# A two-layer decoder trunk on one core: two early requests moved, the convolution's columns and the token-major copy of x

## The chip, the core and the metric

The kernel runs on one core of a Trainium2 chip. The time is the device time of one execution in microseconds (us), as the median of several executions. Five engines work side by side, each through its own instruction queue in the order in which the program was written: TensorE (PE, with its weight loads shown as PEld), VectorE (DVE), ScalarE (ACT), GpSimd (POOL) and SyncE (SP). SP computes nothing; it only requests transfers. ACT and POOL request some as well.

## What is computed

The reference is a decoder trunk of two layers over 256 tokens of width 1024. The first layer mixes tokens by a causal convolution of 31 taps, the second by block attention; beside both runs a cross-attention into 256 memory tokens. A residual with layer norm, a mixture of 32 experts (two per token) and another residual with layer norm follow. The change touches the first layer alone, before its mixture:

```python
u = jnp.dot(x, conv_w_in[j])
y_mix = conformer_conv(u[..., :2 * MIX_WIDTH], conv_dw_w[j], conv_dw_b[j], conv_ln_g[j], conv_ln_b[j])
q_mem = u[..., 2 * MIX_WIDTH:]
...
y = jnp.dot(jnp.concatenate([y_mix, y_mem], axis=-1), w_o[i])
x = layer_norm(DEEPNORM_ALPHA * x + y, ln1_g[i], ln1_b[i])
```

`conformer_conv` gates one half of its input by the sigmoid of the other, convolves each channel over time, normalises and applies silu.

## The kernel before

All large tiles live in one pool, `big`, of 22 slots of 1 MB (128 partitions by 2048 floats). A slot holds either a weight tile that SP loads or working data that `act` (L150) takes. The list of wanted loads is fixed at the start (L249 to L274), and `pump` (L137) issues the next load at each point of the program where a slot is sure to be free: `act`, `free` and `done` count slots, and a first pass through the whole program finds how many loads may be out at each point. At the start fourteen loads go out: six tiles of `conv_w_in` ("cv"), the memory `memT`, two tiles of `w_mem_kv` with one more of `conv_w_in` between them, and four tiles of `w_o`. The fifteenth, the gains (L189), takes the slot of `hs` of channel block 0 and so waits for `conv(0)`.

Engines work in the order written by hand. `conv_layer` (L541) does, in this order:

- `parted` (L389) splits x transposed (`raw`, loaded at L248) into a rounded part and a rest, by ACT and DVE; then ACT requests the convolution's columns (taps, bias and gains, 204 KB) into the end of the tile `cv` (L552).
- `feed.ahead` and `feed.take` (L350) split weight tiles by halves in the same way: ACT casts (L344), DVE subtracts (L345), and `three` (L400) multiplies 24 times per half on PE (L405). ACT's first cast stands right behind the request for the columns in ACT's queue.
- `glu(b)` (L574) for b = 0, 1, 2 computes a gated projection of 256 channels: two halves into `p_`, two into `g_`, a sigmoid, a product `h` (L594). POOL then writes `h` to DRAM (`hd`, L597) and `shifted` (L612) reads it back eight times, shifted, as `hs` (L617). In `glu(2)`, `conv(0)` and `conv(1)` (L620) stand between the halves of `p_` and those of `g_`.
- `taps(b)` (L556) multiplies the columns into small diagonal blocks `wdg` on POOL. It stands behind `shifted(b)` in POOL's queue. `conv(c)` multiplies `wdg` with `hs` on PE (L626). `last_taps` (L600) does the remaining taps on DVE, from the columns.
- Behind `glu(2)` follow the projection of the memory, `conv(2)`, `conv(3)`, the queries, the attention scores of two heads with `conv(4)`, then `router_load(0)` (four requests on SP, L327 to L331), the token-major copy of x into `xn` (four requests on SP of 256 KB each, L685), the other scores, `conv(5)`, and `residual` (L498), which multiplies `xn` by a scaled identity into the accumulators of the layer's output (L496). Behind it stand the channel means (L694, L695), the values' projection (L405 again) and the variance (L714). DVE subtracts the means at L701.

The mixture `moe(0)` follows, whose 192 tiles of 1 MB stream through the same slots, and then the second layer.

Of the kernel before, what the change touches and what calls it, by code (L numbers as in the profile page):

```python
# [17 lines left out]
S = 256  # L18
D = 1024
NT = S // 128  # L20
# [5 lines left out]
MC = MIX // 128  # L26
CW = 31
# [50 lines left out]
def trunk(tc, *args):  # L78
    trace = body(Blank(), None, *[Blank() for _ in args])
    for i in range(len(trace) - 1, 0, -1):  # L80
        trace[i - 1] = min(trace[i - 1], trace[i])
    body(tc, trace, *args)
# [3 lines left out]
def body(ctx, tc, ahead, xT0, xs, memT, w_mem_kv, conv_w_in, conv_cols, moba_w_in, w_o, gains, w_r,  # L86
          gain_cols, b_rg, b_re, w_gate, w_up, w_down, out):
    nc = tc.nc
# [11 lines left out]
    def pb():  # L100
        return ps.tile([P, 512], F32, name="pb", tag="pb")
# [4 lines left out]
    def t2(name, dt=F32):  # L106
        return wk.tile([P, 512], dt, name=name, tag="t2", bufs=3)
# [38 lines left out]
    def changed():  # L146
        trace.append(NB - use["a"] + use["done"])
        pump()

    def act(name, dt=F32):  # L150
        use["a"] += 1
        changed()
        return big.tile([P, 2048], dt, name=name, tag="big")

    def free(n=1):
        use["a"] -= n
        changed()
# [5 lines left out]
    def want(key, load, gate=None):  # L163
        todo.append((key, load, gate))
# [4 lines left out]
    def done(key):  # L169
        have.pop(key, None)  # L170
        use["done"] += 1
        changed()
# [7 lines left out]
    def load(src, i):  # L180

        def load_(t_):
            nc.sync.dma_start(t_, src[i])
            return t_
        return load_
# [59 lines left out]
    xn = [[keep.tile([P, 512], F32, name=f"xn{t}{h}") for h in range(2)] for t in range(NT)]  # L245
    raw = act("raw")
    for h in range(2):
        nc.sync.dma_start(raw[:, h * 1024:(h + 1) * 1024], xT0[:, h * 1024:(h + 1) * 1024])  # L248
    for b in range(3):  # L249
        for i in range(2):  # L250
            want(("cv", b, i), load(conv_w_in, 2 * b + i))
# [56 lines left out]
    for g, experts in enumerate(plan):  # L308
        for kind, k, n, lo in experts:
            c = NDYN + k if kind == "s" else k  # L310
# [13 lines left out]
    def router_load(l):  # L324
        rws_ = xt([P, 2, J, NL], "rw")
        rw = rws_[:, 0]
        nc.sync.dma_start(rbias[:, :NG], b_rg[l:l + 1])  # L327
        nc.sync.dma_start(rbias[:, 8:], b_re[l:l + 1])
        nc.sync.dma_start(rw, w_r[l])
        gbc = small([P, 2 * J], "gbc")  # L330
        nc.sync.dma_start(gbc, gain_cols[l])  # L331
        rws.append((rw, rws_[:, 1], gbc))
# [208 lines left out]
    def conv_layer():  # L541
        acc = Acc()
        xT = parted(raw, "xT", (nc.scalar.copy, nc.vector.tensor_copy))
        free()
        cv_ = act("cv")
        cv = cv_[:, :MC * S].rearrange("p (c s) -> p c s", c=MC)
        npc, nwr = MC * (CW + 5), MC * 32
        cols = cv_[:, MC * S:MC * S + npc + nwr]
        pct = cols[:, :npc].rearrange("p (c k) -> p c k", c=MC)
        wrc = cols[:, npc:].rearrange("p (c b q) -> p c b q", c=MC, b=4)  # L550
        id32 = cv_[:, 2048 - 32:]
        nc.scalar.dma_start(cols, conv_cols)  # L552
        hd = dr.tile([MC, P * HW], F32, name="hd")
        wdg, hsrc, hs = {}, {}, {}

        def taps(b):  # L556
            w_ = act("wdg").rearrange("p (n c) -> p n c", c=32)
            nc.gpsimd.tensor_tensor(
                w_, wrc[:, 2 * b:2 * b + 2].rearrange("p c b q -> p (c b q)")[:, :, None].to_broadcast(
                    [P, 64, 32]),  # L560
                id32[:, None, :].to_broadcast([P, 64, 32]), op=OP.mult)
            wdg[b] = w_.rearrange("p (i b q) c -> p i b q c", i=2, b=4)
# [6 lines left out]
        def halves(o, xT, n=2):  # L569
            for i in range(2):  # L570
                proj_T(o[:, i * 256:(i + 1) * 256], feed.take(n), xT)
                free()

        def glu(b):  # L574
            p_ = pb()
            halves(p_, xT)
            if b == 0:
                nc.vector.tensor_reduce(id32, ident.rearrange("p (r c) -> p c r", r=4), axis=AX.X, op=OP.add)
            else:
                last_taps(b - 1)  # L580
            if b == 2:
                conv(0)
                conv(1)
            g_ = pb()
            halves(g_, xT)
            sg = t2("sg")
            nc.scalar.activation(sg, g_, AF.Sigmoid)
            hh = (xt, ot)[b]([P, 2, HW], "h") if b < 2 else None
            for i in range(2):
                h = hh[:, i] if b < 2 else t2("h")[:, :HW]  # L590
                nc.gpsimd.memset(h[:, 0:CW - 1], 0.0)
                nc.gpsimd.memset(h[:, CW - 1 + S:], 0.0)
                k = slice(i * S, (i + 1) * S)
                nc.vector.tensor_mul(h[:, CW - 1:CW - 1 + S], p_[:, k], sg[:, k])  # L594
                hsrc[2 * b + i] = h
            for i in range(2):
                nc.gpsimd.dma_start(hd[2 * b + i].rearrange("(p s) -> p s", p=P), hsrc[2 * b + i])  # L597
            shifted(b)

        def last_taps(b):  # L600

            for c in (2 * b, 2 * b + 1):
                o, h = cv[:, c], hsrc.pop(c)
                for k in range(CW - 1, 4 * NQ - 1, -1):
                    w_ = pct[:, c, k:k + 1]
                    if k == CW - 1:
                        nc.vector.tensor_scalar(o, h[:, k:k + S], w_, pct[:, c, CW + 1:CW + 2], op0=OP.mult,
                                                op1=OP.add)
                    else:
                        nc.vector.scalar_tensor_tensor(o, h[:, k:k + S], w_, o, op0=OP.mult, op1=OP.add)  # L610

        def shifted(n):  # L612

            for c in (2 * n, 2 * n + 1):
                hs[c] = act("hs")[:, :4 * HW].rearrange("p (b s) -> p b s", b=4)
                for r in range(4):
                    nc.gpsimd.dma_start(hs[c][32 * r:32 * r + 32, :, :HW - 4],  # L617
                                        view(hd[c, r:], [[HW, 32], [32 * HW, 4], [1, HW - 4]]))

        def conv(c):  # L620
            p_ = pb()
            w_ = wdg[c // 2][:, c % 2]
            h = hs.pop(c)
            for q in range(NQ):
                for b in range(4):
                    nc.tensor.matmul(p_[32 * b:32 * b + 32, :S], lhsT=w_[:, b, q, :],  # L626
                                     rhs=h[:, b, 4 * q:4 * q + S], start=q == 0, stop=q == NQ - 1)
            nc.vector.tensor_add(cv[:, c], p_[:, :S], cv[:, c])
            free(1 + c % 2)
            if 0 < c < MC - 1:  # L630
                nc.vector.tensor_add(csum, cv[:, c], cv[:, 0] if c == 1 else csum)
# [6 lines left out]
        mT = parted(held("mem"), "mT")  # L638
        done("mem")
        taps(1)  # L640
        glu(2)

        p_ = pb()
# [36 lines left out]
        next(ats[0])  # L680
        conv(4)
        router_load(0)
        for t in range(NT):
            for half in range(2):
                nc.sync.dma_start(xn[t][half], xs[t, half])  # L685
        feed.ahead(2)
        next(ats[1])
        conv(5)
# [727 lines left out]

    second = moba_layer()
    moe(0, conv_layer(), second)
    moe(1, second)
    return trace  # L1420
# [56 lines left out]
```

## Time and profile before

| | us |
|---|---|
| median of three runs | 1175.22 |
| the three runs | 1174.49, 1175.22, 1183.54 |
| the profiled execution | 1182.57 |
| its span, from the first to the last instruction | 1180.9 |

The profile shows one execution. PE is busy for 87% of the span, DVE for 31%, ACT for 18%, POOL for 5%. The convolution layer takes roughly the first 140 us. A timeline row gives start, duration, engine, line, operation, what it writes and reads, and in brackets how long the engine had been idle and what released it. Rows of SPq, ACTq and POOL with DMA_DIRECT2D are requests; a transfer itself ends later ("landing").

### The profile page before, as it was taken

Reading aid. Unit: us, or ns where it says so; the run is one execution under the profiler, and the core shown is the slowest. Engines: PE = TensorE matmul, PEld = TensorE weight load, DVE = VectorE, ACT = ScalarE, POOL = GpSimd, SP = SyncE. Lnnn points to the kernel's source line nnn. Section 1 sums busy time; section 2 is a strip of 40 time slices with the busy share of each in tenths; the row PEclk is TensorE's granted clock in tenths of the full one; section 3 lists DMA queues with packets and bytes.
Section 4 is the critical chain, followed back from the end, with each engine's and each line's share of the span. In section 5 each row is a group of like instructions: output and inputs, shape, how many; then the busy total and the mean of one; then the engine's idle time right before and its main releaser. Section 6 shows DMA issues by size and latency. Waiting matters only on the chain. (4 is left out here: it accounts for less than half of the span.)

```text
span 1180.9 us, 26574 instructions
## 1 busy us (share of the span) xinstructions
PE 1028.2 (87%) x11292; PEld 722.3 (61%) x11292; DVE 366.4 (31%) x936; ACT 210.5 (18%) x456; POOL 60.6 (5%) x152
## 2 busy tenths in 40 slices
PE   1998999999889998866589998999997999996775
PEld 1986766665565575544469986666545656654542
DVE  3576832221121121111065765222211211221103
ACT  2314411111010010001044532011010111110000
POOL 1440200000000000000020002000000000000001
PEclk9999989999999999889899997999998999997777
DMA  9686969999999999999997386999999999999994
GB/s 381 235 282 265 347 251 419 424 424 426 425 424 425 427 424 425 426 426 425 425 427 271 108 293 252 384 425 424 426 427 422 425 427 425 424 426 425 426 425 177
DMA packets 63656, 447.16 MB, mean 379 GB/s; under 512 B 7656, under 2 KB 8040, under 8 KB 10280
## 3 DMA queue, kind: packets, MB, share of 16 engines
q1 hardware_dynamic: 61640, 439.73, 90.2%
q0 software_dynamic: 1600, 4.90, 1.5%
q8 instruction: 92, 1.51, 0.5%
q10 hardware_dynamic: 288, 0.73, 0.2%
q14 instruction: 36, 0.29, 0.1%
HBM read 442.87 MB, written 2.46 MB: 377 GB/s over the span
## 5 line engine op out<-in xcount | busy, mean ns | idle before, releaser
L974 PE MATMUL pb<-w,xg 128*32 128x128 f32 (+2 forms) x6528 | 400.1, 323 | 87.3 <-DMA w<-in_w_gate_dram 51.0
L974 PEld LDWEIGHTS pb<-w,xg 128*32 128x32 f32 (+2 forms) x6528 | 276.6, 123 | 208.9 <-issue 82.8
L1026 PE MATMUL pb<-w,hT 128*32 128x256 f32 (+1 forms) x1600 | 157.5, 432 | 7.8 <-DMA w<-in_w_down_dram 3.1
L1026 PEld LDWEIGHTS pb<-w,hT 128*32 128x32 f32 (+1 forms) x1600 | 74.5, 116 | 62.9 <-issue 36.5
L1031 ACT COPY o<-pb 32x256 f32<-32x256 f32 (+2 forms) x104 | 43.2, 416 | 367.1 <-DVE o L1031 232.5
L405 PE MATMUL pb<-xT,hl 128*128 128x256 f32 x672 | 86.0, 290 | 25.8 <-ACT hl L344 25.6
L1031 DVE COPY o<-pb 32x256 f32<-32x256 f32 (+2 forms) x104 | 49.8, 478 | 177.6 <-PE pb L1026 157.7
L998 DVE TENSOR_TENSOR h<-pb,h 128x128 f32<-128x128 f32 (+2 forms) x64 | 22.9, 358 | 253.8 <-PE pb L974 246.8
L405 PEld LDWEIGHTS pb<-xT,hl 128*128 128x128 f32 x672 | 84.0, 198 | 27.3 <-ACT hl L344 25.6
L496 PE MATMUL pa<-o,pt 128*128 128x512 f32 x192 | 92.7, 628 | 3.5 <-DVE o L1031 2.0
L950 PEld LDWEIGHTS pb<-oh,xn 128*128 128x128 f32 x704 | 80.6, 192 | 7.4 <-issue 7.4
L950 PE MATMUL pb<-oh,xn 128*128 128x128 f32 x704 | 84.0, 278 | 0.0
L345 DVE TENSOR_TENSOR hl<-w,hl 128x1024 fp32r<-128x1024 f32 x53 | 63.1, 1221 | 36.0 <-ACT hl L344 33.1
L496 PEld LDWEIGHTS pa<-o,pt 128*128 128x128 f32 x192 | 37.7, 207 | 44.5 <-issue 32.4
L344 ACT CAST hl<-w 128x1024 fp32r<-128x1024 f32 x54 | 54.7, 1053 | 33.3 <-DMA w<-in_memT_dram 19.3
L992 ACT ACTIVATE h<-pb 128x128 f32<-128x128 f32 (+2 forms) x64 | 21.2, 331 | 195.9 <-PE pb L974 195.0
L128 POOL TENSOR_SCALAR lmv<-lmv 128x1 f32<-128x1 f32 x8 | 1.7, 216 | 1027.7 <-DVE lmv L506 1026.0
L496 PE MATMUL pa<-hl,y 128*128 128x512 f32 x192 | 46.0, 395 | 0.0
L125 DVE COPY hT<-pb 128x128 f32<-128x128 f32 (+2 forms) x32 | 11.4, 358 | 105.1 <-PE pb L1004 81.2
L123 ACT COPY xg<-pb 128x512 f32<-128x512 f32 x22 | 12.9, 586 | 160.4 <-PE pb L950 160.4
L496 PEld LDWEIGHTS pa<-hl,y 128*128 128x128 f32 x192 | 35.5, 188 | 8.0 <-issue 0.5
L1238 DVE TENSOR_SCALAR ow<-iota,sm,sw 128x128 f32<-128x128 f32 x96 | 26.8, 343 | 19.2 <-PEq L1395 13.3
(229 smaller groups left out, 705.9 us busy)
## 6 DMA issues: line engine op xcount, KB each, us to landing
w<-in_w_gate_dram SPq DMA_DIRECT2D x128, 1024.0 KB, 19.5
w<-in_w_up_dram SPq DMA_DIRECT2D x128, 1024.0 KB, 19.5
w<-in_w_down_dram SPq DMA_DIRECT2D x128, 1024.0 KB, 19.5
w<-in_moba_w_in_dram SPq DMA_DIRECT2D x10, 1024.0 KB, 18.4
w<-in_w_o_dram SPq DMA_DIRECT2D x8, 1024.0 KB, 19.8
w<-in_conv_w_in_dram SPq DMA_DIRECT2D x7, 1024.0 KB, 15.4
w<-in_gains_dram SPq DMA_DIRECT2D x4, 1024.0 KB, 12.4
hs<-hd POOLq DMA_DIRECT2D x24, 142.0 KB, 3.2
```

The costliest lines, as they stand in the source:

```text
L123: nc.scalar.copy(o, i)
L344: nc.scalar.copy(hi, src)
L345: eng.tensor_sub(lo, src, hi.bitcast(F32))
L405: nc.tensor.matmul(o, lhsT=lhs(a, j), rhs=rhs(b, j), start=k == 0, stop=k == 3 * n - 1)
L496: nc.tensor.matmul(self.at[t][half], lhsT=lhsT, rhs=rhs, start=start, stop=stop)
L950: nc.tensor.matmul(p_[:, j - jj], lhsT=now(t, j), rhs=oh[t], start=t == 0, stop=t == NT - 1)
L974: nc.tensor.matmul(o_[b * n:(b + 1) * n, :], lhsT=self.xs[:, j, :], rhs=wj[:, pairs(b) if fw == P else slice(b * fw, (b + 1) * fw)], start ...
L992: nc.scalar.activation(self.h[:, :fw], g_, AF.Silu)
L998: nc.vector.tensor_mul(self.h[:, :fw], u_, self.h[:, :fw])
L1026: nc.tensor.matmul(ds[0][b * n:(b + 1) * n, :dw], lhsT=chunk(c), rhs=wd(c, b * dw, (b + 1) * dw), start=c == 0, stop=c == 3)
L1031: (nc.scalar.copy if 2 * b >= m else nc.vector.tensor_copy)(o[lo:lo + n, b * D // m:(b + 1) * D // m], ds[b] if nb == 1 else ds[0][b * n:( ...
L1238: nc.vector.tensor_scalar(o_[:, t], iota, sm[:, i:i + 1], sw[:, 4 + i:5 + i], op0=OP.is_equal, op1=OP.mult)
```

## The change

Two requests move; nothing is added or removed. The tile `cv` is taken, and its columns are requested by ACT, right after x is requested and before any weight tile is. The four requests for `xn` on SP move from behind `router_load(0)` to ahead of `glu(2)`. The number of slots in use is the same from `conv_layer`'s first steps on, so the loads are issued at the same points of the program.

```diff
     raw = act("raw")
     for h in range(2):
         nc.sync.dma_start(raw[:, h * 1024:(h + 1) * 1024], xT0[:, h * 1024:(h + 1) * 1024])
+    cv_ = act("cv")
+    ncol = MC * (CW + 5), MC * 32
+    nc.scalar.dma_start(cv_[:, MC * S:MC * S + sum(ncol)], conv_cols)
     for b in range(3):
         for i in range(2):
             want(("cv", b, i), load(conv_w_in, 2 * b + i))
...
         xT = parted(raw, "xT", (nc.scalar.copy, nc.vector.tensor_copy))
         free()
-        cv_ = act("cv")
         cv = cv_[:, :MC * S].rearrange("p (c s) -> p c s", c=MC)
-        npc, nwr = MC * (CW + 5), MC * 32
-        cols = cv_[:, MC * S:MC * S + npc + nwr]
...
-        nc.scalar.dma_start(cols, conv_cols)
...
         taps(1)
+        for t in range(NT):
+            for half in range(2):
+                nc.sync.dma_start(xn[t][half], xs[t, half])
         glu(2)
...
         conv(4)
         router_load(0)
-        for t in range(NT):
-            for half in range(2):
-                nc.sync.dma_start(xn[t][half], xs[t, half])
         feed.ahead(2)
```

## Rows read from the trace of the kernel before

**Rows 1.** The page's 40 slices: GB/s moved in each slice of 29.5 us.
```profile
GB/s 381 235 282 265 347 251 419 424 424 426 425 424 425 427 424 425 426 426 425 425 427 271 108 293 252 384 425 424 426 427 422 425 427 425 424 426 425 426 425 177
```
**Rows 2.** Waits, 0 to 180 us: total us, times, longest.
```profile
ACT hl L344 <- DMA w<-in_memT_dram: 19.3, 1, 19.3
```
**Rows 3.** Timeline of all engines, 0 to 70 us: the start.
```profile
4.87 0.78 SPq L183 DMA_DIRECT2D w<-in_memT_dram  x1
...
9.40 0.33 SPq L183 DMA_DIRECT2D w<-in_conv_w_in_dram  x1
...
14.26 7.74 SPq L183 DMA_DIRECT2D w<-in_w_o_dram  x4
24.09 0.38 ACTq L552 DMA_DIRECT2D cv<-in_conv_cols_dram  x1
24.50 5.78 ACT L344 CAST hl<-w 128x1024 fp32r<-128x1024 f32 x6 [19.27 <-DMA w<-in_memT_dram]
...
25.60 31.77 PE L405 MATMUL pb<-xT,hl 128*128 128x256 f32 x240 [25.60 <-ACT hl L344]
```
**Rows 4.** DMA requests by tile: count, KB each, median us to landing.
```profile
hs<-hd POOLq DMA_DIRECT2D x24, 142.0 KB, 3.2
...
w<-in_memT_dram SPq DMA_DIRECT2D x1, 1024.0 KB, 19.2
...
cv<-in_conv_cols_dram ACTq DMA_DIRECT2D x1, 204.0 KB, 7.0
```
**Rows 5.** Windows: length, busy us of PE, PEld, DVE, ACT, POOL; PEclk, DMA share, GB/s.
```profile
20.00:30.00 10.00, 4.40 (x20) 4.40 (x21) 4.42 (x4) 5.50 (x6) 0.00 (x0) 1.00 1.01 425
30.00:40.00 10.00, 10.00 (x79) 10.00 (x78) 2.77 (x4) 1.56 (x2) 0.00 (x0) 1.00 1.01 428
...
41.00:42.00 1.00, 1.00 (x11) 1.00 (x10) 0.82 (x3) 1.00 (x2) 0.20 (x1) 1.00 0.09 25
...
100.00:105.00 5.00, 5.00 (x8) 2.02 (x9) 2.34 (x3) 0.77 (x1) 0.00 (x0) 0.66 0.64 240
```
**Rows 6.** Timeline of all engines, 69 to 150 us: PE ahead of and behind the residual.
```profile
99.82 5.40 PE L496 MATMUL pa<-xn,alpha 128*128 128x512 f32 x8 [3.25 <-DMA xn<-in_xs_dram]
...
105.06 0.59 PE L694 MATMUL pb<-csum,avg 128*128 128x256 f32 x2
...
105.73 6.10 PE L405 MATMUL pb<-hl,mT 128*128 128x256 f32 x48
```
**Rows 7.** Timeline of all engines, 0 to 70 us: the first convolution's supply.
```profile
41.80 1.33 POOL L597 DMA_DIRECT2D hd<-h  x2 [37.95 <-DVE h L594]
...
44.72 4.49 POOL L617 DMA_DIRECT2D hs<-hd  x8 [1.57 <-ACT hl L344]
...
49.23 3.67 POOL L558 TENSOR_TENSOR wdg<-cv 128x2048 f32<-128x2048 f32 x1
...
57.30 6.25 PE L626 MATMUL pb<-hs,wdg 128*32 128x256 f32 x112
...
60.59 0.33 SPq L189 DMA_DIRECT2D w<-in_gains_dram  x1
```
**Rows 8.** Tile hs, requests of 75 to 78 us: time to landing.
```profile
DMA to landing us min/median/max: 4.6/7.8/8.0
```
**Rows 9.** Timeline of all engines, 69 to 150 us: SP's requests beside those hs.
```profile
75.28 6.57 SPq L213 DMA_DIRECT2D w<-in_w_up_dram  x2
```
**Rows 10.** PEld's timeline, 99 to 106 us: the last two of eight loads.
```profile
103.77 0.19 PEld L496 LDWEIGHTS pa<-xn,alpha 128*128 128x128 f32 x1 [0.25 <-issue]
104.20 0.19 PEld L496 LDWEIGHTS pa<-xn,alpha 128*128 128x128 f32 x1 [0.24 <-issue]
```
**Rows 11.** Timeline of all engines, 69 to 150 us: DVE and ACT behind the means.
```profile
99.99 2.35 DVE L345 TENSOR_TENSOR hl<-w,hl 128x1024 fp32r<-128x1024 f32 x2
...
106.12 1.08 DVE L701 TENSOR_TENSOR cv<-cv,pb 128x256 f32<-128x256 f32 x3 [3.78 <-PE pb L695]
...
109.48 0.42 ACT L703 ACTIVATE sq<-cv 128x256 f32<-128x256 f32 x1 [0.25 <-DVE cv L701]
```

More of the change, by code (lines that the diff above doesn't have):

```diff
@@ L544, in conv_layer @@
         free()
-        cv_ = act("cv")
         cv = cv_[:, :MC * S].rearrange("p (c s) -> p c s", c=MC)
-        npc, nwr = MC * (CW + 5), MC * 32
-        cols = cv_[:, MC * S:MC * S + npc + nwr]
-        pct = cols[:, :npc].rearrange("p (c k) -> p c k", c=MC)
-        wrc = cols[:, npc:].rearrange("p (c b q) -> p c b q", c=MC, b=4)
+        cols = cv_[:, MC * S:MC * S + sum(ncol)]
+        pct = cols[:, :ncol[0]].rearrange("p (c k) -> p c k", c=MC)
+        wrc = cols[:, ncol[0]:].rearrange("p (c b q) -> p c b q", c=MC, b=4)
         id32 = cv_[:, 2048 - 32:]
-        nc.scalar.dma_start(cols, conv_cols)
         hd = dr.tile([MC, P * HW], F32, name="hd")
```

## Prediction

> **What bounds the kernel now.** I read the page's slices first. From the seventh slice (177 us) to the end, but for a dip between the mixtures, the transfers run at 419 to 427 GB/s [rows 1]: the mixtures are bound by the stream of expert tiles, and in the first six slices, where this change lies, they are not (235 to 381). What the convolution layer saves should therefore reach the end whole: the stream that follows keeps its length and starts earlier, since its requests are released by slots that this layer frees.
>
> Then the waits of the first 180 us. The longest one in front of a moved request is ACT's: 19.3 us before its first cast, by the profile for `memT` [rows 2]; PE's wait for `xn` comes below. The timeline shows what ACT's wait is. ACT's cast stands behind the columns' request, and that comes at 24.09; the cast follows at 24.50 and PE's first matmul at 25.60 [rows 3]. The cast reads a `conv_w_in` tile, not `memT`. It is the request in front of it that waits: `memT` was requested at 4.87 and took 19.2 us [rows 3, 4], so it landed at 24.07, 0.02 us ahead. Counting the requests of SP and ACT together in program order, `memT` is the 9th and the columns are the 17th. SP's 11th comes at 9.40 and its 13th to 16th start at 14.26, spread over 7.74 us [rows 3], about 2.45 us apart, which is what one tile of 1.05 MB takes at 428 GB/s [rows 5]. I read from this that a request waits for the landing of the one eight places before it; then the 11th shows the landing of the 3rd, which is the first weight tile, at 9.40.
>
> PE is the limit from 25.60 to 57.37, without a gap: 240 matmuls, 48 to a weight tile, so 6.35 us per tile of which one lands every 2.45 us [rows 3].
>
> Later PE waits 3.25 us at L496 for `xn`, until 99.82, so it was free at 96.57 [rows 6]. That also costs clock: in 100 to 105 us the granted clock is 0.66, where 30 to 40 us has 1.00 [rows 5].
>
> **The columns.** As third request they wait for no landing. The request itself (0.38 us of ACT) falls in ACT's wait for x. Their 204 KB take 0.49 us at 428 GB/s ahead of the first weight tile, which then lands at 9.89 instead of 9.40. The cast follows at once, and the first matmul 1.10 us after the cast (24.50 to 25.60) [rows 3]: PE starts at 11.0, 14.6 us earlier. If the columns delay the tile by nothing, it is 15.1; if by twice their size, 14.1. Later tiles come faster than PE uses them, so all 240 matmuls move by as much, and would end at 42.8. In program order there are seventeen hardware requests up to here as before, and those behind wait for landings long past.
>
> The cover that this takes away is that of POOL's round trip. In the profile, `h` goes out at 41.80, when the weight tiles have just run out: 25 GB/s in 41 to 42 us against 428 ahead of it [rows 5, 7]. Moved by 14.6 us it goes out at 27.2, into a stream that lasts until 41.2, and until about 43.7 with `xn` behind it (2.45 us, below). Nearest rows for a transfer in such a stream: the columns themselves took 7.0 us for 204 KB with tiles queued around them, and the `hs` requests of 75 to 78 us, with an expert tile requested at 75.28, up to 8.0 [rows 4, 8, 9]; the median of `hs` is 3.2. In the profile the second `hd` needs about 2.2 us (second request at about 42.5, `hs` from 44.72). `wdg` is ready at 52.90 and `conv(0)` starts at 57.30: 4.4 us of slack [rows 7]. With 7.0 us for `hd` the slack falls to -0.4; with 5.5, which I take since `hd` is smaller than the columns, to 1.1: `hs` requested from 33.5 to 38.0, `wdg` at 41.7, `conv(0)` at 42.7. The last `hs`, requested at 37.5, lands by 45.5 even at 8.0, and `conv(1)` wants it at 45.9. For small delays of DVE's work, which POOL's product now meets elsewhere, I take 0.5, with 0 and 1.6 as ends. Blocks 1 and 2 have slack of their own: the second set of `hs` is wanted by `conv(2)`, behind a whole `glu`.
>
> **xn.** Its four requests pass the fifteenth load, the four of `router_load` and eight tiles of the first experts on SP. SP stands idle from 22.0 to 60.59 there, because the gains wait for `conv(0)` [rows 3, 7], so four requests cost SP nothing. They wait for landings of eight before (`memT` and the next three), go out from about 24.5 to 32 behind the last `w_o` tile, and land by 44. The first use is at 96.57 less 14.1, so at 82. PE then runs the eight matmuls without the wait and at full clock. The last two weight loads at full clock are 0.43 us apart [rows 10], so eight take 3.44 us; the matmuls for the means keep their 0.67 (105.06 to 105.73). From 96.57 to the values' projection at 105.73 it is 9.16 us [rows 6], and becomes 4.11: 5.05 us less, of which 3.25 is the wait and 1.80 the clock. If the clock stays low there for another reason, 3.25.
>
> What is late next is DVE: it is occupied with L345 until 102.34 [rows 11], so L701 moves from 106.12 to 102.34, by 3.78 and not by 5.05. But the variance stands behind the 48 matmuls of the projection, which end at 105.73 + 6.10 - 5.05 = 106.8, and the last of ACT's squares, which ended at 109.90, moves with L701 to 106.1 [rows 11]. PE sets the pace with 0.7 us to spare. The megabyte of `xn` also leaves a stretch at 425 GB/s for one in which the queues stood nearly empty; nothing waits on it there, and I count nothing.
>
> **The sum.** 14.6 + 5.05 - 0.5 = 19.1 us. The profiled execution took 1182.57, so 1163.5; it is 7.35 above the median of the three, and against the median of 1175.2 the same sum gives 1156.1.
>
> **Rivals.**
>
> *Turns.* POOL's transfers may get only one turn for each weight tile queued. For it: the `hs` of 75 to 78 us took 8.0 and not 3.2 with few tiles around. Against it: the columns got through seven queued tiles in 7.0 us. Then each of two `hd` waits a turn of 2.45 us, `hs` is requested from about 34.4, four of them land by 45.2, and the rest once the tiles run out at about 44, 0.6 apart. `conv(0)` starts 2.5 us late, and the clock loss behind a wait of that kind was 1.8 at `xn`: 4.3 us off, 1160.4.
> The Trainium skill's page "DMA: Bandwidth & Descriptors", section "Queues, rings and completion order", says that an engine goes round-robin between queues and drains a whole packet of some 9 to 17 descriptors before it switches. By that rule it would be this rival, 1160.4, against 1156.1 by the columns' row.
>
> *Starved.* POOL's transfers get nothing until the tiles run out at 43.7. Then `hd` lands at about 45.2, `hs` is requested until 49.7, `wdg` is ready at 53.4, and `conv(0)` starts there: 3.9 us earlier than before, less 1.8 of clock, with 5.05 from `xn`: 7.1 in all, 1168. For it: the same `hs` row, of which the median is 7.8. Against it: again the columns.
>
> *The columns were not the wait.* If ACT waits for something else that ends at 24.1, only `xn` counts: 1170.2. Against it stands the 0.02 us.
>
> *Slower.* PE's first 20 matmuls took 4.40 us up to 30, 0.22 each; the next ten microseconds have 79, 0.127 each [rows 5]. If the slow pace belongs to what goes on at the start (tiles streaming in) and not to PE's first steps, all 240 take 52.8 us from 11.0: `conv(0)` at 63.9, 6.6 later than before, less 5.05, and the 112 matmuls of the convolution at that pace some 4.6 more: 1177 to 1181. It decides from about 224 slow matmuls on. Against it: from 30 to 40 us tiles stream in at 428 GB/s beside the fast pace.
>
> **How the numbers follow.** My forecast has 0.58 (1152 to 1160 alone, from the bounds of its terms and the scatter of the runs), turns 0.20, starved 0.14, columns not the wait 0.04, slower 0.04. The prediction is 1156. The range reaches from the forecast's lower end past turns to starved, 1151 to 1168, and leaves out half of starved and the last two. About 1% is what a measurement of this kernel can tell from no change: below 1163.5 lie the forecast and most of turns, 0.73; within 1% starved, the columns case and the rest of turns, 0.24; above it only part of the slow pace, 0.03.
>
> **What would show it.** The columns' request within a microsecond of the start; ACT's first cast at 9.9 and PE's first matmul at 11.0; `hd` requested near 27.2; `conv(0)` near 42.7, where PE's idle time ahead of L626 tells the forecast (0), turns (2 to 3) and starved (over 9) apart; no wait at L496 and a granted clock near 1.00 there; the mixture's first matmul 19 us earlier. It would be wrong if ACT's first cast stays near 24, or if PE loses at L626 what it gained.

## The result and the profile after

The changed kernel takes 1165.88 us against 1181.28 for the kernel before, medians of ten executions each: a ratio of 0.987, with a 95% interval from 0.985 to 0.989. That is 15.4 us, of which the interval leaves 13.0 to 17.8. It is faster by over 1%, and inside the predicted range, but 3.7 us short of the 19.1 that the forecast summed up; the rival called turns (14.8 us, from 1175.2 to 1160.4) is nearer. The predicted 1156 is off by 9.9 us: 6.1 of them because it starts from 1175.2, the median of three runs of the kernel before, where ten gave 1181.28, and the rest is the sum.

PE's timeline of the changed kernel, start and duration first, in brackets how long PE had been idle and what released it (the changed kernel's lines are three later than before from L251 to about L550):

```profile
10.68 31.23 PE L408 MATMUL pb<-xT,hl 128*128 128x256 f32 x240 [10.68 <-ACT hl L347]
45.26 7.94 PE L626 MATMUL pb<-hs,wdg 128*32 128x256 f32 x112 [3.35 <-DMA hs<-hd]
53.12 6.02 PE L408 MATMUL pb<-xT,hl 128*128 128x256 f32 x48
...
86.15 3.70 PE L499 MATMUL pa<-xn,alpha 128*128 128x512 f32 x8
89.69 0.59 PE L694 MATMUL pb<-csum,avg 128*128 128x256 f32 x2
...
90.37 6.10 PE L408 MATMUL pb<-hl,mT 128*128 128x256 f32 x48
```

PE starts at 10.68 and not at 25.60 [rows 3], and the wait at the residual is gone, with its slow matmuls: from L499 to the values' projection it is 4.22 us, where it was 5.91 after a wait of 3.25 [rows 6]. New is the wait of 3.35 us ahead of L626, the convolution of block 0. It takes 7.94 us where it took 6.25 [rows 7].

Subtracting start by start shows where the time came from and where some of it went back:

| start of | before | after | difference |
|---|---|---|---|
| the 240 matmuls | 25.60 | 10.68 | -14.92 |
| `conv(0)` | 57.30 | 45.26 | -12.04 |
| the matmuls behind `conv(1)` | 63.48 | 53.12 | -10.36 |
| the values' projection | 105.73 | 90.37 | -15.36 |
| the mixture's first matmul (L1075) | 138.36 | 123.00 | -15.36 |

ACT's part of the changed kernel's start, in the timeline of all engines. The columns' request comes with the first one of SP, and the first cast at the moment (9.57) at which SP, too, sees the first weight tile landed:

```profile
0.85 0.40 ACTq L251 DMA_DIRECT2D cv<-in_conv_cols_dram  x1
0.85 0.86 SPq L248 DMA_DIRECT2D raw<-in_xT_dram  x2
...
9.57 0.33 SPq L183 DMA_DIRECT2D w<-in_conv_w_in_dram  x1
9.58 1.99 ACT L347 CAST hl<-w 128x1024 fp32r<-128x1024 f32 x2 [3.58 <-DMA w<-in_conv_w_in_dram]
...
24.16 8.94 SPq L643 DMA_DIRECT2D xn<-in_xs_dram  x4
...
26.34 1.34 POOL L597 DMA_DIRECT2D hd<-h  x2 [22.49 <-DVE h L594]
33.07 4.38 POOL L617 DMA_DIRECT2D hs<-hd  x8 [5.40 <-DMA hd<-h]
37.47 3.66 POOL L558 TENSOR_TENSOR wdg<-cv 128x2048 f32<-128x2048 f32 x1
```

Between the second `hd` and the first `hs` POOL waited 1.57 us before [rows 7] and waits 5.40 now, inside the stream of weight tiles. `wdg` is ready at 41.13, before PE needs it; what PE waits for is `hs`. The time to landing of these eight `hs`:

```profile
DMA to landing us min/median/max: 6.3/11.1/12.5
```

The median of `hs` before was 3.2 [rows 4], and 7.8 in its worst stretch [rows 8]. The transfers from 37 to 45 us, by queue (q1 holds SP's requests, q0 POOL's; packets, MB, share of the engines):

```profile
q1 hardware_dynamic: 244, 1.71, 71.4%
q0 software_dynamic: 244, 0.75, 30.5%
```

Packet stands against packet, 244 to 244, so in this stretch neither queue is starved, and not every POOL transfer has to wait for a whole tile. Before it, however, the first one does wait about that long. From 33 to 36 us, with six `hs` requested, the queues carried:

```profile
q1 hardware_dynamic: 176, 1.27, 100.2%
q0 software_dynamic: 3, 0.00, 0.1%
```

The first piece of `hs` goes at 36.8, 3.7 us after the request; in the kernel before it went at 46.0, 1.3 us after. The 2.4 us more are about what a tile takes (2.45 us). `hd` is held up alike: no POOL packet goes between its request at 26.34 and 30 us.

Then the sum of both queues is slow. These are the stretches ahead of and inside the sharing, and that of `conv(0)` (length, busy us of PE, PEld, DVE, ACT, POOL, then granted clock, DMA share, GB/s):

```profile
30.00:36.00 6.00, 6.00 (x53) 6.00 (x52) 3.60 (x6) 0.00 (x0) 2.93 (x6) 1.00 1.01 421
36.00:45.00 9.00, 5.90 (x50) 5.70 (x48) 8.01 (x6) 5.62 (x6) 6.46 (x10) 1.00 1.02 321
45.00:50.00 5.00, 4.75 (x58) 3.13 (x62) 3.22 (x7) 1.05 (x1) 0.00 (x0) 0.66 1.03 317
```

Busy all the time, the queues move 321 GB/s in place of 421. Most of that drop is not the mixing. The `hs` read-backs are slow by themselves: these are the kernel before from 47 to 49 us (255 GB/s) and the last run below from 33 to 37 us (247 GB/s), where nothing but `hs` is on the queues.

```profile
q0 software_dynamic: 165, 0.51, 91.7%
...
q0 software_dynamic: 325, 0.99, 100.7%
```

So 321 lies between `hs` alone and tiles alone. At 255 and 421 GB/s the 0.75 and 1.71 MB of 37 to 45 us would take 2.9 and 4.1 us, 7.0 of the 8 (an estimate from these rows). Only the rest, in which the tiles too move more slowly for their share of the engines (1.71 MB for 71.4% of 8 us, against 2.23 MB for 88.5% of the 6 us from 30 to 36), belongs to the sharing itself.

Behind the wait PE's granted clock is 0.66 on average: it falls from 1.00 (2.4 GHz) to 0.50 (1.2 GHz), and from 50 to 51 us it is 1.00 again:

```profile
47.00:48.00 1.00, 1.00 (x13) 0.55 (x9) 0.88 (x3) 0.00 (x0) 0.00 (x0) 0.50 1.01 286
```

With it the 112 matmuls take 7.94 - 6.25 = 1.69 us more. But the clock alone did not cost that much. `conv(1)` needs the eighth `hs`, which was requested at 36.91, took 12.4 us and landed at 49.3; at full clock PE would have been done with `conv(0)` near 48.4 and would have waited for it, and the matmuls behind `conv(1)`, which takes 3.2 us at full clock, could have started near 52.6 in place of 53.12 (an estimate). So about half a microsecond of the 1.69 is the clock's own, and the rest is again the late `hs`.

### The profile page after: what moved, and what is told of

It is laid out like the page before. It is cut to its first block, busy times and chain, and to the rows that moved or that the text cites. A ratio compares the mean times of both kernels' runs of the same rounds, so it can differ in the third digit from the quotient of the medians.

```text
span 1160.7 us, 26575 instructions
## 1 busy us (share of the span) xinstructions
PE 1025.5 (88%) x11292; PEld 720.9 (62%) x11292; DVE 367.2 (32%) x936; ACT 210.8 (18%) x456; POOL 60.3 (5%) x152
## 5 line engine op out<-in xcount | busy, mean ns | idle before, releaser
L974 PE MATMUL pb<-w,xg 128*32 128x128 f32 (+2 forms) x6528 | 403.7, 325 | 86.3 <-DMA w<-in_w_gate_dram 52.6
L1026 PEld LDWEIGHTS pb<-w,hT 128*32 128x32 f32 (+1 forms) x1600 | 75.3, 117 | 59.9 <-issue 36.8
L499 PE MATMUL pa<-o,pt 128*128 128x512 f32 x192 | 90.0, 613 | 3.5 <-DVE o L1031 2.0
L348 DVE TENSOR_TENSOR hl<-w,hl 128x1024 fp32r<-128x1024 f32 x53 | 67.4, 1302 | 18.0 <-ACT hl L347 15.0
L499 PEld LDWEIGHTS pa<-o,pt 128*128 128x128 f32 x192 | 36.8, 203 | 42.8 <-issue 30.7
L499 PE MATMUL pa<-hl,y 128*128 128x512 f32 x192 | 45.9, 395 | 0.0
L499 PEld LDWEIGHTS pa<-hl,y 128*128 128x128 f32 x192 | 35.5, 188 | 7.9 <-issue 0.5
```

The source lines that it names most:

```text
L348: eng.tensor_sub(lo, src, hi.bitcast(F32))
L499: nc.tensor.matmul(self.at[t][half], lhsT=lhsT, rhs=rhs, start=start, stop=stop)
L974: nc.tensor.matmul(o_[b * n:(b + 1) * n, :], lhsT=self.xs[:, j, :], rhs=wj[:, pairs(b) if fw == P else slice(b * fw, (b + 1) * fw)], start ...
L1026: nc.tensor.matmul(ds[0][b * n:(b + 1) * n, :dw], lhsT=chunk(c), rhs=wd(c, b * dw, (b + 1) * dw), start=c == 0, stop=c == 3)
```

## Experiments

**Each half alone.** The theory after the result: the columns' early request gives 15 us at PE's start, the sharing of the queues takes 5 back, and the early copy of x gives 5. The first run keeps the copy of x where it was, the second one the columns' request.

```diff
 # columns alone, against the changed kernel
         taps(1)
-        for t in range(NT):
-            for half in range(2):
-                nc.sync.dma_start(xn[t][half], xs[t, half])
         glu(2)
...
         router_load(0)
+        for t in range(NT):
+            for half in range(2):
+                nc.sync.dma_start(xn[t][half], xs[t, half])
```

> Only the columns' request moves; the copy of x stays where it was. Theory: PE starts at 10.7 us, conv(0) waits about 3.3 us for hs as in the changed kernel, since the copy of x stands behind the last w_o tile and the fourth hs (45.1 us) lands ahead of it; later PE waits some 3 us for xn and loses 1.8 us of clock. Some 10 us faster than before, ratio 0.991 to 0.992. Rival (the megabyte of xn in the stream is what holds hs back): conv(0) waits less than 1 us and 13 to 15 us are gained, ratio 0.987 to 0.989.

Measured: 1173.44 us, ratio 0.9926 (0.990 to 0.995), 8.7 us faster. PE's waits (total us, times, longest):

```profile
PE pb L408 <- ACT hl L347: 10.2, 1, 10.2
PE pa L499 <- DMA xn<-in_xs_dram: 5.2, 1, 5.2
PE pb L626 <- DMA hs<-hd: 4.7, 2, 3.7
```

The wait for `hs` is there without the megabyte of `xn` behind the weight tiles: 4.7 us in two parts, where the second profile of the changed kernel (below) has 5.1. So `xn` is not what holds `hs` back. The wait for `xn` has grown from 3.25 to 5.2 us: the gain of the columns alone is partly lost there, and is 8.7 us where some 10 were expected.

> Only the four requests for xn move; ACT still asks for the columns behind its first copy. Theory: PE starts at 25.6 us as before, conv(0) does not wait, the wait of 3.25 us at the residual and its slow clock go, the values' projection starts 5.0 us earlier; 5 us faster, ratio 0.9957. Rival (DVE takes the wait's place): 3.8 us or less at the variance. Rival (the gain is given back before the mixture): nothing, ratio 0.999 to 1.001.

```diff
 # copy of x alone, against the kernel before
         taps(1)
+        for t in range(NT):
+            for half in range(2):
+                nc.sync.dma_start(xn[t][half], xs[t, half])
         glu(2)
...
         router_load(0)
-        for t in range(NT):
-            for half in range(2):
-                nc.sync.dma_start(xn[t][half], xs[t, half])
```

Measured: 1177.03 us, ratio 0.9961 (0.994 to 0.998), 4.6 us. PE has no wait at the residual and none at L626:

```profile
25.41 30.77 PE L405 MATMUL pb<-xT,hl 128*128 128x256 f32 x240 [25.41 <-ACT hl L344]
56.10 6.25 PE L626 MATMUL pb<-hs,wdg 128*32 128x256 f32 x112
...
95.31 3.70 PE L496 MATMUL pa<-xn,alpha 128*128 128x512 f32 x8
```

The term for `xn` stands as summed, 5.05 us, against 4.6 measured. The two halves add up to 13.3 us against 15.4 for both; the intervals of the three runs cover the difference. It would also be expected: once the columns are early, the wait for `xn` that the copy takes away is 5.2 us and not 3.25.

**What ACT waited for.** The prediction put ACT's wait down to the request's place in ACT's queue and not to the columns' late landing. Here POOL requests them, at the old place in the program:

```diff
-        nc.scalar.dma_start(cols, conv_cols)
+        nc.gpsimd.dma_start(cols, conv_cols)
```

> The kernel before, with the columns requested at the old place in the program but by POOL in place of ACT. Theory (what cost 15 us was that ACT stood behind a request that waited for memT's landing, and not that the columns came late): ACT's first cast is released by the first weight tile near 9.5 us and PE starts near 10.6 us, as in the changed kernel. Rival (the columns' landing itself holds the start, or ACT waits for memT for another reason): PE starts at 25 us still.

Measured once: 1172.58 us. The timeline:

```profile
7.75 0.78 POOL L552 DMA_DIRECT2D cv<-in_conv_cols_dram  x1 [4.08 <-issue]
9.25 1.99 ACT L344 CAST hl<-w 128x1024 fp32r<-128x1024 f32 x2 [4.04 <-DMA w<-in_conv_w_in_dram]
10.35 30.70 PE L405 MATMUL pb<-xT,hl 128*128 128x256 f32 x240 [10.35 <-ACT hl L344]
45.36 4.63 PE L626 MATMUL pb<-hs,wdg 128*32 128x256 f32 x56 [4.31 <-DMA hs<-hd]
```

PE starts at 10.35 though the columns are asked for 7 us later than in the changed kernel, behind eight tiles. The 15 us were the price of one request standing in front of ACT's casts, not of the columns. The wait for `hs` comes with the early start here too. The time is that of a single run; what the experiment shows is read from the timeline.

**What `hs` waits for.** If it is the sharing of the queues with weight tiles, tiles that are not needed yet must not be asked for until `hs` is through. The four `w_o` tiles (first needed behind the residual) now wait for a small POOL memset that stands behind the eight requests for `hs` of block 0:

```diff
+    def load_behind(src, i):
+        def load_(t_):
+            nc.gpsimd.memset(t_[:, 0:1], 0.0)
+            nc.sync.dma_start(t_, src[i])
+            return t_
+        return load_
...
-        want(("wo", 0, b), load(w_o, b))
...
+            want(("wo", 0, b), load_behind(w_o, b), "wo")
...
             shifted(b)
+            if b == 0:
+                opened("wo")
```

> The changed kernel, with the four w_o tiles (4 MB) requested only once POOL has issued the eight hs of block 0 (each request waits for a small POOL memset of its tile behind them). Theory (hd and hs share the queues with the weight tiles): the stream ends near 31 us, hd lands by 32 and the last hs by 41 us, conv(0) follows the 240 matmuls at 41.9 us without a wait and takes 6.25 us and not 7.94; some 5 us faster than the changed kernel, ratio to before 0.983. Rival (hs is slow by itself at that place, as DVE's work beside it delays POOL's requests): the wait of 3.3 us stays, ratio 0.987.

Measured: 1165.12 us, ratio 0.9869 (0.984 to 0.990): no faster than the changed kernel, where 5 us were expected. PE's timeline shows why:

```profile
10.16 31.29 PE L418 MATMUL pb<-xT,hl 128*128 128x256 f32 x240 [10.16 <-ACT hl L357]
41.38 6.25 PE L638 MATMUL pb<-hs,wdg 128*32 128x256 f32 x112
...
60.85 3.23 PE L638 MATMUL pb<-hs,wdg 128*32 128x256 f32 x56 [1.52 <-DMA hs<-hd]
67.62 6.00 PE L638 MATMUL pb<-hs,wdg 128*32 128x256 f32 x56 [3.54 <-DMA hs<-hd]
```

Block 0 does as the theory says: no wait, 6.25 us, and the time to landing of `hs` (first line) is what it is on empty queues. But the `w_o` tiles now share the queues with `hs` of block 1 (second line), and `conv(2)` and `conv(3)` wait 5.06 us together, with a slow clock behind the second wait (6.00 us for the 56 matmuls, 3.23 ahead of it). That weight tiles on the same queues make `hs` late is shown, by taking it away at one place and meeting it at another.

```profile
DMA to landing us min/median/max: 2.8/3.1/4.8
...
DMA to landing us min/median/max: 7.5/11.8/15.7
```

**Following the wait.** Next the changed kernel ran again, and beside it one with the same tiles behind the `hs` of block 1 (`if b == 1` in place of `if b == 0` in the diff above).

> The changed kernel once more, for the comparison with the next one on the same chip: ratio 0.987, conv(0) waits 3.3 us for hs, its first 56 matmuls slow, no wait at the residual.

Measured: 1164.52 us, ratio 0.9862 (0.983 to 0.990), as the first time. PE's timeline differs from the first one in a way that tells what ends the wait:

```profile
44.20 4.55 PE L626 MATMUL pb<-hs,wdg 128*32 128x256 f32 x56 [3.95 <-DMA hs<-hd]
49.86 3.23 PE L626 MATMUL pb<-hs,wdg 128*32 128x256 f32 x56 [1.11 <-DMA hs<-hd]
53.02 6.01 PE L408 MATMUL pb<-xT,hl 128*128 128x256 f32 x48
```

`conv(0)` starts 1.06 us earlier than in the first profile, and `conv(1)` then waits 1.11 us for the last `hs`; the matmuls behind it start at 53.02, against 53.12. What PE gains ahead of the last `hs` it loses waiting for it.

> As the run with the w_o tiles behind the first hs, but they are requested only once POOL has issued the hs of block 1 (near 47 us). Theory (hd and hs suffer from whatever tiles share the queues with them, and the earlier try only moved the wait from block 0 to block 1): conv(0) and conv(2) start without a wait, the values' projection at about 85.5 us against 90.4 in the changed kernel; ratio to before 0.9825, some 5 us faster than the changed kernel. Rival (the wait moves on to block 2, since eight tiles are then requested between 45 and 52 us): conv(4) waits 3 to 6 us for hs, ratio 0.986 to 0.988. Rival (tiles asked for later are missed by the mixture): conv(4) does not wait, and the mixture's first matmul gains less than 2 us of the 5.

Measured: 1165.77 us, ratio 0.986 (0.983 to 0.989). The first rival of the run is right: the wait has moved to block 2, shared between `conv(4)` (1.37 us) and `conv(5)` (2.06).

```profile
74.57 3.23 PE L638 MATMUL pb<-hs,wdg 128*32 128x256 f32 x56 [1.37 <-DMA hs<-hd]
...
80.92 3.23 PE L638 MATMUL pb<-hs,wdg 128*32 128x256 f32 x56 [2.06 <-DMA hs<-hd]
84.08 3.70 PE L509 MATMUL pa<-xn,alpha 128*128 128x512 f32 x8
```

The residual comes 2.1 us earlier than in the changed kernel, too little for the measurement.

**The streams kept apart.** The last one leaves all three blocks alone: x's copy and one `w_o` tile behind the `hs` of block 0, three `w_o` tiles behind those of block 1, the gains and so all the experts' tiles behind those of block 2. `behind` puts a small POOL memset ahead of a load, as `load_behind` did.

```diff
-        want(("wo", 0, b), load(w_o, b))
-    want(("gb", 0, 1), load_gb(0))
...
+    for n_, b in enumerate((3, 0, 1, 2)):
+        want(("wo", 0, b), behind(load(w_o, b)), "hs1" if n_ else "hs0")
+    want(("gb", 0, 1), behind(load_gb(0)), "hs2")
...
             shifted(b)
+            if b == 0:
+                for t in range(NT):
+                    for half in range(2):
+                        nc.gpsimd.memset(xn[t][half][:, 0:1], 0.0)
+                        nc.sync.dma_start(xn[t][half], xs[t, half])
+            opened(f"hs{b}")
...
         taps(1)
-        for t in range(NT):
-            for half in range(2):
-                nc.sync.dma_start(xn[t][half], xs[t, half])
         glu(2)
```

> The changed kernel, with every large transfer kept out of the way of all three blocks' hd and hs: x's copy and one w_o tile are requested behind the hs of block 0, the other three w_o tiles behind those of block 1, the gains and with them all tiles of the experts behind those of block 2 (each behind a small POOL memset of its tile). Theory (what the changed kernel loses is the sharing of the queues, wherever it falls): no wait at any conv, no wait at the residual, the residual at about 81 us against 86.1 in the changed kernel, ratio to before 0.9825. Rival (the experts' tiles, now 6 to 15 us later, are missed by the mixture): the residual at 81 us but the mixture's last tile as in the changed kernel, ratio 0.986 or more.

Measured: 1158.10 us, ratio 0.9824 (0.980 to 0.985), 20.8 us in place of 15.4. PE's timeline, and the time to landing of all 24 `hs`:

```profile
10.17 30.60 PE L414 MATMUL pb<-xT,hl 128*128 128x256 f32 x240 [10.17 <-ACT hl L353]
40.70 6.25 PE L638 MATMUL pb<-hs,wdg 128*32 128x256 f32 x112
...
58.58 6.25 PE L638 MATMUL pb<-hs,wdg 128*32 128x256 f32 x112
...
72.52 3.23 PE L638 MATMUL pb<-hs,wdg 128*32 128x256 f32 x56
...
80.25 3.70 PE L505 MATMUL pa<-xn,alpha 128*128 128x512 f32 x8
```
```profile
DMA to landing us min/median/max: 2.7/3.2/4.9
```

No `conv` waits for `hs`, and the residual comes 5.9 us earlier than in the changed kernel. The mixture's first matmul comes 5.15 earlier (117.85 against 123.00) and the span of the profiled execution is 5.8 shorter, so the experts' tiles, asked for later, are not missed. It is faster than the kernel before, and in all likelihood than the changed one: four of its five times lie below every one of the changed kernel's sixteen, and its interval ends where that of the first measurement of the changed kernel begins, though the second one's (0.983 to 0.990) overlaps it.

## Why the prediction was right, and where it was not

**The columns.** Right in mechanism and size. PE was to start at 11.0 and starts at 10.68, 14.92 us earlier against 14.6 summed. That ACT waited behind its own request, and that this request waited for the landing of the one eight places before it, was read from one coincidence of 0.02 us; the run with POOL's request shows the first half of it directly. The count of eight was argued from the spacing of SP's requests. The changed kernel's trace bears it out, with every place behind the columns moved by one. The `conv_w_in` request that was the 11th is the 12th, and still goes out when the first weight tile, now the 4th, has landed (9.57). `memT`, now the 10th, is requested at 5.31 and takes 18.8 us, so it lands at 24.11, and the 18th, the first of `xn`, goes out at 24.16.

**POOL's round trip.** Here the forecast failed. The place was right (`conv(0)`, because `hd` and `hs` fall into the stream of tiles), and the size was not: it allowed 0.5 us, with 1.6 as the upper end, and the profile shows 3.35 of wait and 1.69 of clock, 5.04 together. The step that failed is "the last `hs`, requested at 37.5, lands by 45.5 even at 8.0". It took the worst time to landing in the trace as a bound for each of eight requests. In that stretch only one tile stood beside them; in the changed kernel they meet tiles all along. The first piece goes out 2.4 us later than before, and the landings lie 0.4 to 2.4 us apart, where the requests lie 0.55 us apart. `conv(0)` needs the first four: the fourth, requested at 34.7, took 10.4 us, landed at 45.1 and released PE at 45.26. The eighth, requested at 36.91, took 12.4 and landed at 49.3. `hd` was taken at 5.5 and took 6.1 to 6.5. The second part, the clock, was priced for the rivals and left out of the forecast's own range. That the range held all the same is because it reached past the forecast to two rivals.

**The rivals.** Turns gave 2.5 us of wait, 1.8 of clock and 14.8 us in all; measured were 3.35, 1.69 and 15.4. Its numbers come near, and its mechanism holds for the start alone: the first piece of `hs` does go out about a tile's time later. If each `hs` waited for a whole tile, the queues' packets in 37 to 45 us could not stand 244 to 244 (and 219 to 216 in the run with the columns alone). The counts fit packets that take turns one by one, and what then makes `hs` slow is that its own packets move at some 250 GB/s even alone, and tiles' packets stand between them. Starved, which had POOL wait until the tiles run out, is excluded by the same rows. Why the read-backs are slow is open: `hs` reads from DRAM what `hd` has just written, in small pieces from shifted places, and no run varied any of it. Small pieces alone do not explain it: from 30 to 36 us the packets of `hd`, as small but going the other way, into DRAM, took 12.2% of the engines for 0.30 MB, a pace of 410 GB/s.
The Trainium skill's page "DMA: Bandwidth & Descriptors", section "Queues, rings and completion order", says that an engine goes round-robin between queues, which the equal counts bear out. It also says that an engine drains a whole packet of some 9 to 17 descriptors before it switches. A tile's share of one engine is some 8 pieces here (1.05 MB in pieces of 8 KB, 16 engines), so that would be about a whole tile at each turn: the late first piece would fit it, the equal counts behind it do not bear it out.

**xn.** Right: no wait at L499, full clock, and 5.0 us (10.36 behind `conv(1)` to 15.36 at the projection) against 5.05 summed. The copy alone measured 4.6. That `xn` would land by 44 did not come true: the first of its transfers took 25.8 us and landed at 50. It cost nothing, since PE wants `xn` at 86.15.

**The way to the end.** That the convolution layer's gain reaches the end whole holds within the scatter: 15.4 us at the values' projection and at the mixture's first matmul (19 were forecast), and 15.4 between the medians. The profiled executions differ by 20.2 us in span, more than the medians; single executions scatter by several us, so that difference says nothing of its own.

In short, 14.92 and 5.0 for the two parts, 0.5 from the 240 matmuls themselves (31.23 against 31.77), and 5.04 back at `conv(0)` and `conv(1)`: 15.4. The 0.5 is luck: these matmuls took between 30.3 and 31.8 us in the profiles, whether they started early or late.

## What to carry to other kernels

A request in a compute engine's queue is part of that engine's work: if it has to wait for an earlier transfer, everything behind it waits too. Where the first instruction of an engine starts exactly at the landing of a tile that it does not read, look for the request in front of it.

When a stage starts earlier, its small transfers move as well, and may leave the empty queues that had made them quick. The price of a chain of small transfers in a full stream is not the worst single time to landing in the trace, since each waits for the ones ahead of it as well as for the stream; ask also what pace they reach alone. And prefetches that are not urgent can be tied behind them.

## What the runs showed of the hardware that I had not expected

- POOL's `hs` read-backs kept the queues 92 to 101% busy at 247 to 255 GB/s with nothing beside them. While they shared the queues with SP's 1 MB tiles, the packet counts of both queues were equal, and the queues, busy all the time, moved 321 GB/s in place of 421. Eight `hs` then took up to 12.5 us to land each, and up to 15.7 in the run with the tiles behind the first `hs`, against 2.8 to 4.8 on nearly empty queues.
- A POOL transfer that was requested while tiles were queued sent its first piece about 2.4 us later than on empty queues (3.7 against 1.3 us behind the request).
- A wait of PE can cost clock behind it. At the residual before, the matmuls behind a wait of 3.25 us took 5.40 us in place of 3.70. At `conv(0)`, behind 3.35 us, they took 1.69 longer, most of which, by the estimate above, PE would otherwise have waited for `hs`. Behind waits of 1.52 us (tiles behind the first `hs`), 1.37 and 2.06 us (tiles behind the second) the 56 matmuls ran at full pace, 3.23 us.
